# Attention steps queued behind weight splits, and attention heads placed anew among the weight pieces

## The chip, the cores and the metric

The kernel runs on 1 core of one Trainium2 chip. A time is that of one execution of the whole program on the device, in microseconds (us). The kernel before takes 896.84 us as the median of 3 runs (895.47 to 898.17).

The core's engines run side by side, each through its own queue in order: PE does the matmuls (PEld is its weight load), ACT the exponentials, copies and casts, DVE elementwise work and reductions, POOL a little more elementwise work, and SP issues the DMAs.

## The reference

A bidirectional encoder of two layers, for 256 tokens of width 1024, all in float32:

```python
def _token_mixer(xn, w_in, w_pool, pool_scale, w_a, w_b, w_o, rel_bias):
    u, q, k, v, g_pool, g_attn = jnp.split(xn @ w_in, SPLITS, axis=-1)
    # pooling: centred means over 2/4/8/16 tokens, minus the token, times w_pool and a scale
    ...
    # attention: 12 heads of 128 in 3 groups of dilation 1, 4, 16; +-64 strided keys; a bias per head
    ...
    wts = jax.nn.softmax(jnp.stack(lses, axis=0), axis=0)      # groups weighed by their sums
    attn = jnp.einsum('gbsh,gbshd->bshd', wts, jnp.stack(outs, axis=0))
    merged = jax.nn.sigmoid(g_pool) * (pool_out @ w_a) + jax.nn.sigmoid(g_attn) * (attn_out @ w_b)
    return merged @ w_o

def reference(x, ...):
    h = x
    for layer in range(DEPTH):
        h = h + _token_mixer(_rmsnorm(h, norm1[layer]), ...)
        h = h + _conv_ffn(_rmsnorm(h, norm2[layer]), ...)      # width-3 convolution, GELU, gate
    return _rmsnorm(h, norm_f)
```

The weights are float32 and are all read once, 178.68 MB from memory by the profile.

## The kernel before

**Weights in two halves.** Products are made from a high half and a low half of each operand, three matmuls for each block of 128 x 512. A weight is loaded in loads of 1 MB or so into one of three buffers (`raw`), and each load holds two *pieces*. A piece is split: ACT casts its high half, `wh` (L206), and DVE subtracts that from the raw weight, `wl` (L208). There are five buffers for pieces, and a piece takes the one that the piece five before it leaves. `W.get()` hands out the next piece and writes the splits up to three pieces ahead; the load of raw weights behind them is written at once too, on SP's queue (L143). In the stage of this change a piece is used by `by_tokens`, 12 matmuls of 128 x 512 (`v_sum`, L688), and four pieces make one step of 512 columns.

**The order.** The instructions are written in the program's order, but a scheduler places them on each engine: an instruction goes when its inputs are expected, by the scheduler's own costs. Only an edge keeps two in order. `W.after_splits()` gives every instruction of its block an edge to the last high half on ACT and to the last low half on DVE that are written by then (`self.last`). A chip's engine then takes its instructions strictly in the order they were placed.

**The attention between the pieces.** In each layer the projections to queries and keys take 24 pieces, with two of the pooling mixer's among them (numbers 20 to 45 in layer 0), the output of the pooling mixer 8 (46 to 53), the first gate 8 (54 to 61) and the second gate with `w_b` 12 (62 to 73). After each of the 40 pieces of the projections, the pooling output and the first gate `step()` is called, and a table, `steps`, says which parts of the attention are written there. Four *heads* here are the four slots of a group; each slot does its head of all three groups at once:

- `scores(hh)`: for each half of the tokens, matmuls for the near keys (L1054) and for the two strided groups (L1060) into one PSUM tile; DVE scales and adds the bias (L1065) and takes the maximum, negated (`nm`, L1070); ACT does the exponential and its sum (L1073); DVE inverts the sum (L1075) and scales (L1076).
- `start_turn(hh)`: DVE transposes the probabilities in blocks (L735), and SP writes them to memory and reads them back turned (L739, L744).
- `turn(hh)`: ACT and DVE split the turned rows (`pth`, `ptl`: L1096, L1097).
- `weigh(hh)`: 6 matmuls (L1106) and 4 in plain float32 (L1110; the profile shows each of these, and of those of L1060, as two) with the values; ACT and DVE evict the result in two halves (`at2`: L1115, L1116).
- `bring(half)` copies queries out of the rows that came back turned (L1135).

The copies of the pooling mixer's product, `pa` (L1192), and the gates' tanh (L1198) lie between them.

Of the kernel before, what the change touches and what calls it, by code (L numbers as in the profile page):

```python
# [10 lines left out]
F32 = mybir.dt.float32  # L11
F32R = mybir.dt.float32r
AF = mybir.ActivationFunctionType
ALU = mybir.AluOpType
# [7 lines left out]
HD = 128  # L22
# [224 lines left out]
def encoder(ctx, tc, x, w_in, w_pool, pool_scale, w_a, w_b, w_o, norm1, norm2, w_up, conv_w,  # L247
            conv_b, w_down, rel_bias, norm_f, onehot, edges, out):
    nc = tc.nc
# [9 lines left out]
    W = Weights(tc, wpool, big)  # L259

    def cols(w, c0):

        src = w[:, c0 : c0 + 256].rearrange("(k p) c -> p k c", p=P)
        return W.add(
            src, (8, 256), [((lambda t, j=j: t[:, :, j * P : (j + 1) * P]), (8, P)) for j in (0, 1)]
        )
# [26 lines left out]
    for l in range(DEPTH):  # L293
# [37 lines left out]
        for f in range(4, NF, 2):  # L331
            if f in HALF_GROUPS:
                n, j = HALF_GROUPS[f]
                W.use(rows(w_up[l], j * 512, 4, DFF + n * 512, 512))
            a = cols(w_up[l], f * P)
            if f >= 4 * NQ:
                g = cols(w_up[l], DFF + f * P)
                a = [a[0], g[0], a[1], g[1]]
# [107 lines left out]
    def bias_of(t, hh):  # L446

        b = bt[:, hh]
        (pstep, pn), _ = b.ap
        blocks, first = (-2 * P, 4 * P - 1) if t == 0 else (-3 * P, 5 * P - 1)  # L450
        return bass.AP(b.tensor, b.offset + first, [[pstep, pn], [blocks, 2], [-1, 256]])
# [227 lines left out]
    def v_tile():  # L679
        return acc.tile([P, 512], F32, tag="acc", name="v_ps")  # L680
# [248 lines left out]
    for l in range(DEPTH):  # L929
# [25 lines left out]
        else:  # L955
            for g in range(NG):
                held = begun[0] if g == 0 else [W.get() for _ in range(4)]
                for t in range(2):
                    if g + t == 0:
                        ps = begun[1]  # L960
                    else:
                        ps = v_tile()
# [6 lines left out]
        if l == 0:  # L969
            load_params()  # L970
            with tc.issue_after(W.behind[1].ins):
                bias = build_bias()
# [6 lines left out]
        for gi in range(3, -1, -1):  # L979
# [10 lines left out]
            cur, n = u, S + 2 * PAD  # L990
            sh = 1
            while sh < w:
# [3 lines left out]
                    out=nxt[:, :, 0:n], in0=cur[:, :, 0:n], in1=cur[:, :, sh : sh + n]  # L996
# [7 lines left out]
            if hw > 1:  # L1004
# [5 lines left out]
                out=pd, in0=cur[:, :, o : o + S], scalar=1.0 / w, in1=u[:, :, PAD : PAD + S],  # L1010
                op0=ALU.mult, op1=ALU.subtract,
# [37 lines left out]
        def scores(hh):  # L1049
            for t in range(2):  # L1050
                ps = acc.tile([P, 512], F32, tag="acc", name="s_ps")
                ql, kl = (lows[hh // 2][:, j, hh % 2] for j in range(2))
                for m, (a, b) in enumerate(((qh[:, hh], kh[:, hh]), (qh[:, hh], kl), (ql, kh[:, hh]))):
                    nc.tensor.matmul(  # L1054
                        ps[:, 0:256], a[:, t, :], b.rearrange("p t m -> p (t m)"),
                        start=(m == 0), stop=(m == 2),
                    )
                for g in (1, 2):
                    c = 2 * (g - 1) + hh % 2
                    nc.tensor.matmul(  # L1060
                        ps[:, 128 + g * 128 : 256 + g * 128], q[:, hh // 2, c, t, :],
                        kk[:, hh // 2, 4 * t : 4 * t + 4, c, :], start=True, stop=True,
                    )
                s = sm.tile([P, 512], F32, tag="s", name="s")
                nc.vector.scalar_tensor_tensor(  # L1065
                    out=s.rearrange("p (a b) -> p a b", a=2), in0=ps.rearrange("p (a b) -> p a b", a=2),
                    scalar=HD**-0.5, in1=bias_of(t, hh), op0=ALU.mult, op1=ALU.add,
                )
                nm = sm.tile([P, 1], F32, tag="nm", name="nm")
                nc.vector.tensor_reduce(out=nm, in_=s, axis=AX.X, op=ALU.max, negate=True)  # L1070
                z = sm.tile([P, 1], F32, tag="z", name="z")
                p = sm.tile([P, 512], F32, tag="p", bufs=3, name="p")
                nc.scalar.activation(p, s, AF.Exp, bias=nm[:, 0:1], accum_out=z)  # L1073
                rz = sm.tile([P, 1], F32, tag="rz", name="rz")
                nc.vector.reciprocal(rz, z)  # L1075
                nc.vector.tensor_scalar(  # L1076
                    out=p, in0=p, scalar1=rz[:, 0:1], scalar2=0.5, op0=ALU.mult, op1=ALU.mult
                )
                probs[hh, t] = p
# [20 lines left out]
        def weigh(hh):  # L1100
            pth, ptl, pt = ptiles[hh]
            ps = acc.tile([P, 2, P], F32, tag="acc", name="o_ps")
            for kc in range(2):
                c = slice(hh * P, (hh + 1) * P)
                for m, (a, b) in enumerate(((vh, pth), (vh, ptl), (vl, pth))):
                    nc.tensor.matmul(ps, a[:, kc, c], b[:, kc], start=(kc + m == 0), stop=False)  # L1106
            for g in (1, 2):
                hd = (g - 1) * HPG + hh
                for t in range(2):
                    nc.tensor.matmul(  # L1110
                        ps[:, t, :], v[:, t, hd * P : (hd + 1) * P], pt[:, 4 * t : 4 * t + 4, 1 + g, :],
                        start=False, stop=(g == 2 and t == 1),
                    )
            oh, ol = at2[:, hh, 0], at2[:, hh, 1]
            nc.scalar.copy(out=oh, in_=ps)  # L1115
            nc.vector.tensor_sub(out=ol, in0=ps, in1=oh.bitcast(F32))  # L1116

        def parts(which):

# [11 lines left out]
        def bring(half):  # L1131
# [8 lines left out]
            12: ((parts, 1),),  # L1140
            16: ((bring, 0),),
            21: ((scores, 0), (start_turn, 0)),
            24: ((bring, 1),),
            25: ((scores, 1), (start_turn, 1)),
            28: ((turn, 0),),
            29: ((weigh, 0), (scores, 2), (start_turn, 2)),
            32: ((turn, 1),),
            33: ((weigh, 1), (scores, 3), (start_turn, 3)),
            36: ((turn, 2),),
            37: ((weigh, 2),),  # L1150
            38: ((turn, 3),),

            39: ((weigh, 3), (W.load_one, first_up[l][1])),
# [10 lines left out]
        for n in range(6):  # L1164
# [3 lines left out]
            ps = by_tokens(x2, 4, then=step, ahead=pool_out(po2) if n == 1 else None)  # L1168
            y = tmp[:, 1].rearrange("p (t q c j) -> p t q c j", t=2, q=4, c=4)
            if n in (2, 4):  # L1170
                z = tmp[:, 0].rearrange("p (a c j) -> p a c j", a=8, c=4)
            else:

                z = kk[:, (1, 0, None, 0, None, 1)[n]]
# [12 lines left out]
        pa = []  # L1187
        for n in range(2):
            ps = by_tokens(po2, 4, then=step)
            pa.append(big.tile([P, 2, 512], F32, tag=("q0", "k0")[n], name="pa"))  # L1190
            for t in range(2):
                nc.scalar.copy(out=pa[n][:, t], in_=ps[t])  # L1192

        def gate(tag):
            ps = by_tokens(x2, 4, then=step if steps else None)
# [5 lines left out]
        for n in range(2):  # L1201
            th = gate("q1")
            for t in range(2):
                nc.vector.scalar_tensor_tensor(
                    out=pa[n][:, t], in0=th[:, t], scalar=1.0, in1=pa[n][:, t],
                    op0=ALU.add, op1=ALU.mult,
# [8 lines left out]
        for n, cc in enumerate(HALVES):  # L1215
            th = gate("gates")
            ps = by_tokens(at2, 2, 2)
            ks = slice(4 * n, 4 * n + 4)
            y = turned_rows[:, n]
            z = big.tile([P, 2, 4, 4, 32], F32, tag=("q1", "v0")[n], name="merged")  # L1220
            for t in range(2):

                with tc.issue_after((turning if t else made[1]).ins) if n + t else ExitStack():
                    nc.vector.scalar_tensor_tensor(
                        out=th[:, t], in0=th[:, t], scalar=1.0, in1=ps[t], op0=ALU.add, op1=ALU.mult
# [187 lines left out]
```

## Time and profile before

| | |
|---|---|
| median of 3 runs | 896.84 us |
| the profiled execution, its own time | 895.75 us |
| its span, first to last instruction | 893.9 us |
| PE busy | 862.6 us (97%) |
| DVE busy | 658.7 us (74%) |
| ACT busy | 483.9 us (54%) |
| split, DVE (L208), 274 times | 329.1 us, 1216 ns each |
| split, ACT (L206), 274 times | 282.9 us, 1050 ns each |
| mean granted clock of PE | 0.992 |

The page gives the engines' busy times; a view by stretches of time gives the same for any stretch. A timeline lists instructions in order: start, duration, engine, line, operation, output and inputs; `x2` are merged neighbours, and the brackets at the end give how long the engine stood idle before it and what ended that. PE's matmuls are pipelined: one of 128 x 512 lasts about 390 ns while the next starts some 227 ns after it.

### The profile page before, as it was taken

The numbers are of one execution on the slowest core, as the hardware profiler recorded it, in microseconds if no ns is written. First come the engines' busy times: TensorE is split into PE (matmuls) and PEld (weight loads), VectorE is DVE, ScalarE is ACT, GpSimd is POOL, SyncE is SP. The second block draws the span as 40 slices with busy tenths as digits, with TensorE's granted clock in tenths as the row PEclk, the third lists the DMA queues.
The fourth block names the chain that finished last, engine by engine and source line by source line (L and its number), as shares of the span: only waits on it lengthen the run. The fifth ranks groups of instructions, "written<-read, shape, count | busy, mean of one in ns | idle before, by whom it ended". The sixth has DMA issues, their size and how long they took to land.

```text
span 893.9 us, 11515 instructions
## 1 busy us (share of the span) xinstructions
PE 862.6 (97%) x4151; PEld 721.4 (81%) x4151; DVE 658.7 (74%) x1018; ACT 483.9 (54%) x759; POOL 31.0 (3%) x98
## 2 busy tenths in 40 slices
PE   9999997899999999999999999888999999999997
PEld 7888886677888888888888888766778888888886
DVE  7998736655866878989856986374668677888884
ACT  7756524335544565766644664152554464765673
POOL 1800000000010000000000000000000100000000
PEclk9999999999999999999999999999999999999999
DMA  9678675658765777666726578667576568776741
GB/s 329 203 242 274 223 259 163 212 174 279 288 224 189 264 250 262 203 223 232 236 95 219 160 258 282 212 182 240 178 283 226 210 220 273 248 247 214 242 157 47
DMA packets 153089, 199.37 MB, mean 223 GB/s; under 512 B 6905, under 2 KB 101825, under 8 KB 153033
## 3 DMA queue, kind: packets, MB, share of 16 engines
q1 hardware_dynamic: 152872, 198.38, 66.4%
q8 instruction: 32, 0.52, 0.2%
q10 hardware_dynamic: 160, 0.27, 0.1%
q14 instruction: 25, 0.20, 0.1%
HBM read 178.68 MB, written 19.94 MB: 222 GB/s over the span
## 4 chain that ended last, share of the span: by engine, by line
PE 89%; DVE 4%; ACT 3%; DMA 2%; issue 1%; SPq 0%; POOL 0%; POOLq 0%; ACTq 0%; DVEq 0%
PE t_ps L688 40%; PE proj_ps L564 17%; PE v_ps L688 6%; PE res_ps L608 6%; PE res_ps L607 6%; PE res_ps L606 6%; PE v_ps L921 2%; DVE wl L208 2%; PE pool_ps L564 1%; PE v_ps L828 1%; ACT wh L206 1%; DMA turned_p<-turning 1%; PE o_ps L1110 1%; DMA turning<-turning 1%; PE o_ps L1106 1%
## 5 line engine op out<-in xcount | busy, mean ns | idle before, releaser
L208 DVE TENSOR_TENSOR wl<-raw,wh 128x1024 fp32r<-128x1024 f32 x274 | 329.1, 1216 | 82.3 <-ACT wh L206 79.4
L206 ACT CAST wh<-raw 128x1024 fp32r<-128x1024 f32 x274 | 282.9, 1050 | 118.6 <-PE t_ps L688 59.5
L688 PE MATMUL t_ps<-wh,x 128*128 128x512 f32 x960 | 303.2, 393 | 5.7 <-ACT wh L206 5.7
L688 PEld LDWEIGHTS t_ps<-wh,x 128*128 128x128 f32 x960 | 180.9, 189 | 44.2 <-ACT wh L206 6.5
L688 PE MATMUL t_ps<-wl,x 128*128 128x512 f32 x480 | 189.7, 395 | 3.5 <-DVE wl L208 3.5
L688 PEld LDWEIGHTS t_ps<-wl,x 128*128 128x128 f32 x480 | 91.0, 190 | 25.5 <-DVE wl L208 6.7
L564 PE MATMUL proj_ps<-x,wh 128*128 128x512 f32 x448 | 106.5, 390 | 0.0
L564 PEld LDWEIGHTS proj_ps<-x,wh 128*128 128x128 f32 x448 | 83.1, 188 | 16.6
L607 PE MATMUL res_ps<-wl,actq 128*128 128x512 f32 (+1 forms) x184 | 70.0, 380 | 0.0
L608 PE MATMUL res_ps<-wh,actk 128*128 128x512 f32 (+1 forms) x184 | 69.9, 380 | 0.0
L606 PE MATMUL res_ps<-wh,actq 128*128 128x512 f32 (+1 forms) x184 | 69.8, 381 | 0.0
L564 PEld LDWEIGHTS proj_ps<-x,wl 128*128 128x128 f32 x448 | 56.9, 191 | 1.9
L564 PE MATMUL proj_ps<-x,wl 128*128 128x256 f32 x448 | 57.5, 283 | 0.0
L688 PE MATMUL t_ps<-wh,po 128*128 128x512 f32 x128 | 42.7, 408 | 8.2 <-ACT wh L206 8.2
L1065 DVE SCALAR_TENSOR_TENSOR s<-s_ps,bt 128x512 f32<-128x512 f32 x16 | 10.8, 685 | 41.5 <-PE s_ps L1060 41.5
L608 PEld LDWEIGHTS res_ps<-wh,actk 128*128 128x128 f32 x184 | 34.6, 188 | 6.6
L607 PEld LDWEIGHTS res_ps<-wl,actq 128*128 128x128 f32 x184 | 34.6, 188 | 6.4
L606 PEld LDWEIGHTS res_ps<-wh,actq 128*128 128x128 f32 x184 | 34.5, 188 | 6.3
L1073 ACT ACTIVATE p<-s,nm 128x512 f32<-128x512 f32 x16 | 11.6, 725 | 50.6 <-DVE nm L1070 49.6
L688 PEld LDWEIGHTS t_ps<-wh,po 128*128 128x128 f32 x128 | 25.2, 199 | 14.4 <-ACT wh L206 9.4
L1115 ACT CAST at<-o_ps 128x256 fp32r<-128x256 f32 x8 | 3.0, 372 | 52.9 <-PE o_ps L1110 35.0
L475 POOL TENSOR_SCALAR ss<-ss 128x1 f32<-128x1 f32 x8 | 2.0, 254 | 817.6 <-ACT junk L468 817.6
(199 smaller groups left out, 1151.9 us busy)
## 6 DMA issues: line engine op xcount, KB each, us to landing
raw<-in_w_up_dram SPq DMA_DIRECT2D x44, 1024.0 KB, 7.2
raw<-in_w_in_dram SPq DMA_DIRECT2D x34, 1024.0 KB, 5.5
raw<-in_w_in_dram SPq DMA_DIRECT2D x50, 512.0 KB, 4.5
raw<-in_w_down_dram SPq DMA_DIRECT2D x22, 1024.0 KB, 6.0
raw<-in_w_a_dram SPq DMA_DIRECT2D x8, 1024.0 KB
raw<-in_w_o_dram SPq DMA_DIRECT2D x8, 1024.0 KB, 4.9
crossing<-qk_rows SPq DMA_DIRECT2D x12, 512.0 KB, 5.6
crossing<-crossing SPq DMA_DIRECT2D x12, 512.0 KB, 6.0
```

Of the source, the lines that this page charges most:

```text
L206: inst = nc.scalar.copy(out=h, in_=src)
L208: inst = nc.vector.tensor_sub(out=l, in0=src, in1=h.bitcast(F32))
L564: nc.tensor.matmul(out, w(k), x, start=(steps is first and k == 0), stop=(steps is last and k == nk - 1), skip_group_check=turns["rest"],)
L606: nc.tensor.matmul(ps, ah, wh, start=first, stop=False, skip_group_check=on)
L607: nc.tensor.matmul(ps, ah, wl, start=False, stop=False, skip_group_check=on)
L608: nc.tensor.matmul(ps, al, wh, start=False, stop=last, skip_group_check=on)
L688: nc.tensor.matmul(ps, x2[:, 2 * n + j, part, t, :], w[:, j, :], start=(n + m == 0), stop=(n == last and m == 5),)
L828: return nc.tensor.matmul(ps[t], a[:, k, t, :], w[:, k % 2, :], start=first, stop=last)
L921: nc.tensor.matmul(ps[t], a[:, k, t, :], w[:, j, :], start=(k + m == 0), stop=(k == KD - 1 and m == 2),)
L1065: nc.vector.scalar_tensor_tensor(out=s.rearrange("p (a b) -> p a b", a=2), in0=ps.rearrange("p (a b) -> p a b", a=2), scalar=HD**-0.5, in1 ...
L1073: nc.scalar.activation(p, s, AF.Exp, bias=nm[:, 0:1], accum_out=z)
L1106: nc.tensor.matmul(ps, a[:, kc, c], b[:, kc], start=(kc + m == 0), stop=False)
```

## The change

Three kinds of attention instructions now get the edges of `after_splits`: the bias addition, the exponential, and the evictions of the weighing and of `pa`. And the table of `steps` writes scores and weighing at other pieces.

```diff
-                nc.vector.scalar_tensor_tensor(
-                    out=s.rearrange("p (a b) -> p a b", a=2), in0=ps.rearrange("p (a b) -> p a b", a=2),
-                    scalar=HD**-0.5, in1=bias_of(t, hh), op0=ALU.mult, op1=ALU.add,
-                )
+                with W.after_splits():
+                    nc.vector.scalar_tensor_tensor(
+                        out=s.rearrange("p (a b) -> p a b", a=2), in0=ps.rearrange("p (a b) -> p a b", a=2),
+                        scalar=HD**-0.5, in1=bias_of(t, hh), op0=ALU.mult, op1=ALU.add,
+                    )
...
-                nc.scalar.activation(p, s, AF.Exp, bias=nm[:, 0:1], accum_out=z)
+                with W.after_splits():
+                    nc.scalar.activation(p, s, AF.Exp, bias=nm[:, 0:1], accum_out=z)
...
-            nc.scalar.copy(out=oh, in_=ps)
-            nc.vector.tensor_sub(out=ol, in0=ps, in1=oh.bitcast(F32))
+            with W.after_splits():
+                nc.scalar.copy(out=oh, in_=ps)
+                nc.vector.tensor_sub(out=ol, in0=ps, in1=oh.bitcast(F32))
...
-            24: ((bring, 1),),
-            25: ((scores, 1), (start_turn, 1)),
-            28: ((turn, 0),),
-            29: ((weigh, 0), (scores, 2), (start_turn, 2)),
-            32: ((turn, 1),),
-            33: ((weigh, 1), (scores, 3), (start_turn, 3)),
-            36: ((turn, 2),),
-            37: ((weigh, 2),),
+            24: ((scores, 1), (start_turn, 1)),
+            25: ((bring, 1),),
+            27: ((turn, 0),),
+            28: ((weigh, 0), (scores, 2), (start_turn, 2)),
+            30: ((turn, 1),),
+            31: ((weigh, 1), (scores, 3), (start_turn, 3)),
+            35: ((turn, 2),),
+            36: ((weigh, 2),),
             38: ((turn, 3),),
             39: ((weigh, 3), (W.load_one, first_up[l][1])),
...
-                nc.scalar.copy(out=pa[n][:, t], in_=ps[t])
+                with W.after_splits():
+                    nc.scalar.copy(out=pa[n][:, t], in_=ps[t])
```

The line numbers of the attention rise by up to four in the changed kernel (L1073 becomes L1075).

Outside the attention's stretch of each layer every engine's order is the same. Three places in layer 0 follow; layer 1 reads alike.

On ACT, where the scores of heads 0 and 1 are done and the pooling output begins (pieces 46 to 50; `p`, `z` are the probabilities and their sums). Before:

```order
L206 CAST wh45_1299<-raw22_1195 128x1024
L1073 ACTIVATE p_1344,z_1343<-s_1339,nm_1341 128x512
L206 CAST wh46_1315<-raw23_1241 128x1024
L1073 ACTIVATE p_1360,z_1359<-s_1355,nm_1357 128x512
L206 CAST wh47_1374<-raw23_1241 128x1024
L206 CAST wh48_1390<-raw24_1275 128x1024
L206 CAST wh49_1419<-raw24_1275 128x1024
L1073 ACTIVATE p_1465,z_1464<-s_1460,nm_1462 128x512
L1073 ACTIVATE p_1481,z_1480<-s_1476,nm_1478 128x512
L1192 COPY pa_1529<-t_ps_1417 128x512
L1135 COPY q_791<-qk_rows_793 128x1024
L1192 COPY pa_1529<-t_ps_1418 128x512
```

Now:

```order
L206 CAST wh45_1299<-raw22_1195 128x1024
L206 CAST wh46_1315<-raw23_1241 128x1024
L206 CAST wh47_1374<-raw23_1241 128x1024
L206 CAST wh48_1390<-raw24_1275 128x1024
L206 CAST wh49_1419<-raw24_1275 128x1024
L1075 ACTIVATE p_1344,z_1343<-s_1339,nm_1341 128x512
L1075 ACTIVATE p_1360,z_1359<-s_1355,nm_1357 128x512
L1075 ACTIVATE p_1446,z_1445<-s_1441,nm_1443 128x512
L1075 ACTIVATE p_1462,z_1461<-s_1457,nm_1459 128x512
L206 CAST wh50_1476<-raw25_1319 128x1024
L1138 COPY q_791<-qk_rows_793 128x1024
L206 CAST wh51_1495<-raw25_1319 128x1024
```

The casts of pieces 46 to 49 went ahead of all four exponentials, and that of piece 50, which followed the two copies of `pa`, now follows the exponentials directly, ahead of the copies.

On ACT, where head 0 has been weighed and head 2 gets its scores (pieces 53 to 55). Before:

```order
L1096 CAST pth_1550<-turned_p_1049 128x8x2x32
L1115 CAST at2_1416<-o_ps_1572 128x256
L1073 ACTIVATE p_1596,z_1595<-s_1591,nm_1593 128x512
L206 CAST wh54_1554<-raw27_1440 128x1024
L1073 ACTIVATE p_1612,z_1611<-s_1607,nm_1609 128x512
L206 CAST wh55_1626<-raw27_1440 128x1024
```

Now:

```order
L1098 CAST pth_1529<-turned_p_1049 128x8x2x32
L1118 CAST at2_1416<-o_ps_1554 128x256
L1075 ACTIVATE p_1578,z_1577<-s_1573,nm_1575 128x512
L1075 ACTIVATE p_1594,z_1593<-s_1589,nm_1591 128x512
L206 CAST wh54_1608<-raw27_1480 128x1024
L206 CAST wh55_1626<-raw27_1480 128x1024
```

The cast of piece 54 stood between the two exponentials of head 2, and stands behind both now.

On DVE, from the biases of head 1 to the low half of piece 50 (`nm` the maximum, `rz` the inverted sum). Before:

```order
L208 TENSOR_TENSOR wl49_1420<-raw24_1275,wh49_1419 128x1024
L1070 TENSOR_REDUCE nm_1462<-s_1460 128x1
L1065 SCALAR_TENSOR_TENSOR s_1476<-s_ps_1470,bt_82 128x512
L1070 TENSOR_REDUCE nm_1478<-s_1476 128x1
L1075 RECIPROCAL rz_1467<-z_1464 128x1
L1076 TENSOR_SCALAR p_1465<-p_1465,rz_1467 128x512
L1075 RECIPROCAL rz_1483<-z_1480 128x1
L1076 TENSOR_SCALAR p_1481<-p_1481,rz_1483 128x512
L208 TENSOR_TENSOR wl50_1437<-raw25_1319,wh50_1436 128x1024
```

Now:

```order
L208 TENSOR_TENSOR wl49_1420<-raw24_1275,wh49_1419 128x1024
L1066 SCALAR_TENSOR_TENSOR s_1441<-s_ps_1435,bt_82 128x512
L1066 SCALAR_TENSOR_TENSOR s_1457<-s_ps_1451,bt_82 128x512
L1071 TENSOR_REDUCE nm_1443<-s_1441 128x1
L1071 TENSOR_REDUCE nm_1459<-s_1457 128x1
L1077 RECIPROCAL rz_1448<-z_1445 128x1
L1078 TENSOR_SCALAR p_1446<-p_1446,rz_1448 128x512
L1077 RECIPROCAL rz_1464<-z_1461 128x1
L1078 TENSOR_SCALAR p_1462<-p_1462,rz_1464 128x512
L208 TENSOR_TENSOR wl50_1477<-raw25_1319,wh50_1476 128x1024
```

Both biases of head 1 stand behind the low half of piece 49 now; before, the first of them was done ahead of piece 46's.

## The prediction

> **What bounds the kernel now.** I read the page's busy times first, then the stretches of time, then who waited for whom on TensorE (PE), and last the timelines of PE, ScalarE (ACT), VectorE (DVE) and SyncE (SP) around the waits. Pieces of weights are called by their number in the instruction order (`wh50` and `wl50` are the high and low half of piece 50); a time is microseconds from the start of the span, in layer 0.
>
> ```profile
> PE 862.6 (97%) x4151; PEld 721.4 (81%) x4151; DVE 658.7 (74%) x1018; ACT 483.9 (54%) x759; POOL 31.0 (3%) x98
> ...
> 130.00:230.00 100.00, 88.66 (x412) 71.42 (x411) 60.42 (x87) 44.33 (x65) 0.00 (x0) 0.97 0.66 213
> 570.00:670.00 100.00, 88.64 (x413) 71.35 (x412) 59.99 (x86) 44.33 (x65) 0.00 (x0) 0.97 0.66 213
> ...
> 140.00:150.00 10.00, 8.85 (x31) 6.93 (x32) 9.96 (x16) 4.79 (x8) 0.00 (x0) 0.83 0.42 139
> 150.00:160.00 10.00, 7.78 (x33) 5.82 (x32) 5.48 (x9) 7.14 (x10) 0.00 (x0) 1.00 0.75 202
> 170.00:180.00 10.00, 6.63 (x26) 4.99 (x25) 9.33 (x15) 5.82 (x9) 0.00 (x0) 0.83 0.36 134
> ```
>
> PE is the bound: 862.6 of 893.9 us. Its idle time is 31 us, and 22.7 us of that lie in two stretches of 100 us (the columns after the stretch's length are PE, PE weight load, DVE, ACT, POOL, then the granted clock, DMA share and GB/s), one in each layer, where the attention runs between the weight matmuls. DVE is busy 60 and ACT 44 of those 100 us, so neither is short of time: it is a matter of order. The granted clock falls to 0.83 in two slices of 10 us of each stretch.
>
> ```profile
> PE t_ps L688 <- ACT wh L206: 7.9, 4, 2.8
> PE t_ps L688 <- DVE wl L208: 3.4, 7, 0.7
> ...
> 136.12 1.95 PE L1060 MATMUL s_ps<-k,q 128*128 128x128 f32 x16
> 140.48 0.73 PE L688 MATMUL t_ps<-wh,po 128*128 128x512 f32 x2 [2.42 <-ACT wh L206]
> 141.88 0.80 PE L688 MATMUL t_ps<-wl,po 128*128 128x512 f32 x1 [0.66 <-DVE wl L208]
> 145.47 0.62 PE L688 MATMUL t_ps<-wh,po 128*128 128x512 f32 x2
> ...
> 153.65 0.39 PE L688 MATMUL t_ps<-wh,po 128*128 128x512 f32 x1
> 155.74 0.73 PE L688 MATMUL t_ps<-wh,po 128*128 128x512 f32 x2 [1.69 <-ACT wh L206]
> 156.99 0.50 PE L688 MATMUL t_ps<-wl,po 128*128 128x512 f32 x1 [0.52 <-DVE wl L208]
> 157.33 0.63 PE L688 MATMUL t_ps<-wh,po 128*128 128x512 f32 x2
> 165.51 0.28 PE L1106 MATMUL o_ps<-pth,vh 128*128 128x256 f32 x1
> ...
> 169.92 1.05 PE L1060 MATMUL s_ps<-k,q 128*128 128x128 f32 x8
> 173.81 0.73 PE L688 MATMUL t_ps<-wh,x 128*128 128x512 f32 x2 [2.84 <-ACT wh L206]
> 175.07 0.50 PE L688 MATMUL t_ps<-wl,x 128*128 128x512 f32 x1 [0.53 <-DVE wl L208]
> 178.56 0.88 PE L688 MATMUL t_ps<-wh,x 128*128 128x512 f32 x2
> ```
>
> The first two rows are all waits of PE in 130 to 230: 11.3 us, every one for a half of a weight piece, none for the attention itself. Three stops are large. From 157.33 to 165.51 run 36 matmuls without a stop, 0.227 us each, so a piece (12 matmuls) takes 2.73. Stop 1: piece 46 could start at 138.07 and end at 140.80; it ends with the first of the two matmuls at 145.47, about 145.7, so 4.9 are lost, of which the waits are 3.1 and the rest the low clock (0.17 of a slice of 10 us is 1.7). Stop 2: piece 50 could start at 153.88; three of its matmuls are out at 157.33 and nine follow, so it ends at 159.38 instead of 156.61: 2.8 lost, 2.2 as waits, no low clock, 0.3 for each of the two restarts. Stop 3: piece 54 could start at 170.97 and end at 173.70; it ends with the first matmul at 178.56, at about 179.0: 5.3 lost. The other waits are 11.3 - 8.7 = 2.6 in five places; with 0.3 for each restart 4.1. A layer loses about 17.1.
>
> ```profile
> 138.68 0.72 ACT L1073 ACTIVATE p<-s,nm 128x512 f32<-128x512 f32 x1 [16.35 <-DVE nm L1070]
> 139.40 1.03 ACT L206 CAST wh<-raw 128x1024 fp32r<-128x1024 f32 x1
> 152.72 0.59 ACT L1192 COPY pa<-t_ps 128x512 f32<-128x512 f32 x1 [1.83 <-PE t_ps L688]
> 154.63 3.90 ACT L206 CAST wh<-raw 128x1024 fp32r<-128x1024 f32 x4
> 172.01 0.72 ACT L1073 ACTIVATE p<-s,nm 128x512 f32<-128x512 f32 x1 [3.69 <-DVE nm L1070]
> 172.73 1.03 ACT L206 CAST wh<-raw 128x1024 fp32r<-128x1024 f32 x1
> ...
> 136.76 1.29 DVE L1065 SCALAR_TENSOR_TENSOR s<-s_ps,bt 128x512 f32<-128x512 f32 x2 [10.94 <-PE s_ps L1060]
> 137.97 1.27 DVE L1070 TENSOR_REDUCE nm<-s 128x1 f32<-128x512 f32 x2
> 156.86 1.30 DVE L735 STREAM_TRANSPOSE turning<-p 128x512 f32<-128x512 f32 x2
> 158.08 3.46 DVE L208 TENSOR_TENSOR wl<-raw,wh 128x1024 fp32r<-128x1024 f32 x3
> 170.56 0.69 DVE L1065 SCALAR_TENSOR_TENSOR s<-s_ps,bt 128x512 f32<-128x512 f32 x1 [1.78 <-PE s_ps L1060]
> 172.61 0.69 DVE L1070 TENSOR_REDUCE nm<-s 128x1 f32<-128x512 f32 x1
> 175.63 0.45 DVE L1076 TENSOR_SCALAR p<-p,rz 128x512 f32<-128x512 f32 x1
> ```
>
> Each large stop is a cast queued on ACT behind an attention instruction that waits: `wh46` (139.40) behind an exponential that stood 16.35 us for the maximum, `wh50` (154.63) behind the copies of `pa`, which wait for PE's own matmuls, `wh54` (172.73) behind the first exponential of head 2.
>
> **The change, part by part.** It adds and removes no arithmetic; the instruction order differs only in the two attention stretches. DVE steps used below: a low half 1.15 in a row (3.46 for three), bias and maximum 0.64 each in a row, turning a block 0.65, scaling 0.42 when the next starts early.
>
> *Stop 1 goes.* `wh46` to `wh49` now stand ahead of the exponentials and `wl46` ahead of the biases. Their slots come free as pieces 41 to 44 are consumed, before 134, so the casts lie under the matmuls until 138.07. DVE does the biases at 136.76 as before, the maxima to 139.16, `wl47` to 140.35 and `wl48` to 141.5: PE needs `wl47` after piece 46 and two matmuls, at 141.26. It then goes through pieces 46 to 49, from 138.07 to 148.99. Gain 4.9.
>
> *Stop 2 moves.* The exponentials of head 1 now stand ahead of `wh50`, and their biases behind `wl49`. DVE after `wl48`: two reciprocals 0.25, four turnings 2.6 and two scalings 0.85, `wl49` 1.15, two biases 1.28 and two maxima 1.28, hence the last maximum at about 148.8. ACT: the two exponentials start at 148.25 and 149.06 (0.81 with the read of the sum), `wh50` 0.72 after the second, at 149.78, and 1.03 long: PE restarts at 150.86, a wait of 1.87. `wl50` follows to 152.07, so the third matmul comes 1.25 after the first as at 156.99, with a gap of 0.65. Lost: 2.8 (152.12 against 149.44, and 0.1). It was 2.8: no gain and no loss, if the clock stays up as in 150:160.
>
> *Stop 3 grows.* The hold covers only splits that exist when the scores are written; `wh54` is made after them and falls behind both exponentials of head 2. Call T the start of the last score matmuls (169.92 before; 165.05 now, 4.9 earlier). They take 1.05. Before, `wh54` started at T + 2.81. Now the second maximum ends at T + 3.38, as 172.61 + 0.69 says, the second exponential starts at T + 3.42, `wh54` at T + 4.14, and PE at T + 5.22: a wait of 4.17 instead of 2.84. `wl54` comes behind the second scaling and the second turning, at T + 5.7, and the third matmul at T + 6.95 instead of T + 5.15. Behind T + 1.05 + 0.45 that is 5.45, with 0.1 and the low clock (1.7, as at 2.84) 7.25; it was 5.3. Loss 2.0.
>
> *The rest.* From piece 55 on I placed the same steps: all halves are ready before PE needs them, except `wl58`, which stands behind two scalings and two turnings of head 3 and comes 0.35 late, 0.65 with the restart. The five small stops had cost 4.1: gain 3.4. What hides the moved evictions is the distance to the weighing: the closest is head 2, where the low half of the probabilities (now behind `wl59` and the two products with the gate) ends at 191.2 and PE comes to it at 191.3. If that cover goes, each 1 us late costs PE 1 us.
>
> ```profile
> 145.13 0.42 SPq L143 DMA_DIRECT2D raw<-in_w_a_dram  x1
> 155.33 1.78 SPq L744 DMA_DIRECT2D k<-crossing  x4
> 158.19 0.38 SPq L739 DMA_DIRECT2D turning<-turning  x1
> 165.83 1.80 SPq L744 DMA_DIRECT2D turned_p<-turning  x4
> ...
> DMA to landing us min/median/max: 3.4/4.4/5.0
> ...
> DMA to landing us min/median/max: 5.5/5.5/5.5
> ```
>
> The first landing row is that of the turned rows (`turned_p`), the second that of the raw loads from 118 to 200.
>
> *Queues.* On SP a load of raw weights moves behind each turning of heads 1 to 3. Head 1's rows are turned at 153.35, while SP still issues the keys to 157.1, so that the load for piece 54 goes at 157.6 where it went at 157.21 and lands (5.5) at 163, six before its cast. The turned rows of head 1 go by 166.6 even if the 7.6 between 158.19 and 165.83 stays; they land by 171.6 (5.0), and PE asks for them at 177.5. Cost nothing; loads of pieces 58 and 62 go at 171.2 and 187.5 and have seven and more to spare.
>
> *Sum.* A layer: 4.9 + 0 - 2.0 + 3.4 = 6.3; two layers, since 570:670 repeats 130:230, about 13. The profiled execution took 895.75 (span 893.9); the median, 896.84, is 1.1 above it, and carries over: 896.84 - 13 = **883.8 us**.
>
> *The clock.* The 0.83 after a wait of 2.42 and one of 0.66, against 1.00 after 1.69 and 0.52, puts the fall between these; the new 1.87 and 0.65 are nearer the second, so I charge none there and 1.7 at stop 3. Bounds: 0 and 1.7 at either stop. The Trainium skill, "TensorE: Matmul & The Clock Gate", section Part 1: The HAM clock gate (the "warmup" mystery), has the clock halve after an idle window of about 3.4 us and return after a busy one, the windows running free of the program. By that length the new stop 2 would cost nothing and stop 3 the half clock, which is the sum above; yet it would also have spared stop 1, and the trace shows 0.83 there, so the row decides. That the windows run free would make it a matter of where they fall; this is the first rival below.
>
> **The rivals.** *The low clock comes at stop 2 as well* (chance 0.2): two points, 1.69 without and 2.42 with the low clock, do not tell where between them it turns, and 1.87 is between. 1.7 in each layer: 883.8 + 3.4 = 887.2.
>
> *Stop 3 does not grow, and stop 2 neither loses* (0.12): the score matmuls of head 2 end with other work in front that I charged twice, and the small stops were worth the whole floor. Without the 2.0 of stop 3 in both layers: 879.8. Against it: the order of ACT is fixed, and both exponentials stand ahead.
>
> *The stop goes on down the line* (0.08): heads 2 and 3 are weighed with almost no slack (0.1 and 1.4). If the gates' tanh or the turned rows come 2 late, each of the two weighings stops 1 to 2 us and brings the low clock back once; with stop 2's 1.7 that is 3 + 1.7 + 1.7 = 6.4 a layer, all of the gain: 896.6, the same. For it: these steps now wait for PE's own last matmul of a gate. Against it: in 130:230 no wait of PE is for the attention.
>
> *Slower* (0.05): raw loads starve behind the turnings. SP issues in order; three loads a layer now stand behind a turning that waits for DVE. The spare is 6 to 9 us. From a delay of 9 PE waits for each of the three; to lose the gain of 6.3 each must come 2.1 later still, and 14 late would cost 3 x 5 - 6.3 = 8.7 a layer, 914. For it: the stretch before waited 7.6 from turning to turned rows. Against it: turnings end within 6 us of their scores here.
>
> *That the change does nothing* is excluded by the order of ACT: the casts of 46 to 49 do stand ahead.
>
> **How the numbers follow.** The forecast has 0.55: 881 to 886 for single errors of half a microsecond at its ten places. With the rivals: 0.2 at 887, 0.12 at 880, 0.08 at about 896, 0.05 above. The range 877 to 891 leaves out the last two and a little of the edges; of the rival at 896 a quarter falls below the bound of faster. About 0.3% (2.7 us) is what a measurement of this kernel can tell from no change: faster than 894.1 by 0.89, within 0.06, slower 0.05.
>
> **What would show it.** In the profile after: no wait of PE at 138; a wait of about 1.9 for `wh` at 149 and one of about 4.2 at 166, the latter followed by the only slice at 0.83; PE idle near 8 instead of 11.3 in each stretch; the wait of ACT's exponential for the maximum still there, but with no cast behind it that PE needs, save those two. Wrong if PE waits on o_ps, or for a raw load, if the slice after 150 shows 0.83, or if the stop at 166 is below 3.

## The result, and the profile after

The changed kernel takes 882.79 us as the median of 4 runs (882.18 to 884.58), the kernel before 896.19 beside it (895.47 to 898.17): 0.985 of the time, 95% interval 0.983 to 0.987. Predicted were 883.8, within 877 to 891. The profiled execution has a span of 881.5 us, 12.4 less than before.

From the page of the changed kernel, and from its view by stretches (the columns are those of the view before):

```profile
PE 860.3 (98%) x4151; PEld 723.4 (82%) x4151; DVE 660.2 (75%) x1018; ACT 485.9 (55%) x759; POOL 31.9 (4%) x98
...
130.00:230.00 100.00, 93.22 (x441) 77.36 (x440) 66.63 (x91) 46.43 (x68) 0.00 (x0) 0.95 0.72 230
570.00:670.00 100.00, 93.22 (x433) 77.12 (x432) 69.92 (x96) 47.58 (x69) 0.00 (x0) 0.93 0.73 237
...
150.00:160.00 10.00, 9.47 (x35) 7.33 (x34) 6.12 (x7) 4.85 (x7) 0.00 (x0) 0.83 0.73 202
170.00:180.00 10.00, 8.60 (x38) 6.89 (x39) 5.37 (x8) 3.01 (x4) 0.00 (x0) 0.72 0.78 242
580.00:590.00 10.00, 8.14 (x28) 5.95 (x27) 9.25 (x14) 7.73 (x12) 0.00 (x0) 0.83 0.80 241
600.00:610.00 10.00, 5.09 (x13) 3.45 (x13) 9.08 (x14) 4.98 (x8) 0.00 (x0) 0.61 0.48 160
```

PE idles 6.8 us of each attention stretch where it idled 11.3. The granted clock is lower than before, though: 0.95 and 0.93 over the stretches instead of 0.97, with dips at both stops that are left, in both layers. So part of PE's gain in idle time was paid back as slow matmuls.

PE's waits in 130 to 230, and its timeline around the places of the three stops:

```profile
PE t_ps L688 <- ACT wh L206: 5.5, 2, 4.2
PE t_ps L688 <- DVE wl L208: 1.3, 2, 0.8
...
137.12 0.71 PE L688 MATMUL t_ps<-wh,po 128*128 128x512 f32 x2
...
149.63 0.73 PE L688 MATMUL t_ps<-wh,po 128*128 128x512 f32 x2 [1.34 <-ACT wh L206]
...
170.65 1.22 PE L688 MATMUL t_ps<-wh,x 128*128 128x512 f32 x2 [4.16 <-ACT wh L206]
172.62 0.79 PE L688 MATMUL t_ps<-wl,x 128*128 128x512 f32 x1 [0.76 <-DVE wl L208]
```

Piece 46 starts at 137.12 right behind the score matmuls: stop 1 is gone, and so are all small stops (the two rows of waits are two stops and nothing else). Stop 2 has shrunk from 1.69 to 1.34, stop 3 has grown from 2.84 to 4.16. DVE and ACT ahead of stop 2:

```profile
138.46 2.35 DVE L208 TENSOR_TENSOR wl<-raw,wh 128x1024 fp32r<-128x1024 f32 x2
...
145.16 1.28 DVE L1066 SCALAR_TENSOR_TENSOR s<-s_ps,bt 128x512 f32<-128x512 f32 x2
146.36 1.26 DVE L1071 TENSOR_REDUCE nm<-s 128x1 f32<-128x512 f32 x2
...
147.12 0.73 ACT L1075 ACTIVATE p<-s,nm 128x512 f32<-128x512 f32 x1 [7.62 <-DVE nm L1071]
148.55 1.03 ACT L206 CAST wh<-raw 128x1024 fp32r<-128x1024 f32 x1
```

ACT's exponential still stands 7.62 us for the maximum, but the only cast behind it that PE needs is that of piece 50 (148.55).

A simple measure of a layer is the stretch from the start of head 1's score matmuls to the first residual matmul behind the attention. The rows that end it in layer 0, before, and those that begin and end it now:

```profile
241.80 0.39 PE L606 MATMUL res_ps<-wh,m 128*128 128x512 f32 x1
```

```profile
135.42 1.95 PE L1060 MATMUL s_ps<-k,q 128*128 128x128 f32 x16
...
234.67 0.39 PE L606 MATMUL res_ps<-wh,m 128*128 128x512 f32 x1
```

In layer 0 it went from 105.7 us (136.12 to 241.80) to 99.3 (135.42 to 234.67): 6.4 less, where 6.3 were predicted. Layer 1 gave 5.1 (105.7 to 100.6), and 0.7 had been won before layer 0's attention: 12.2 of the 12.4. The second executions of both kernels, further down, give 4.7 in layer 0 (105.2 to 100.5) and 5.4 in layer 1 (104.3 to 98.9), so the close match in layer 0 is in part the luck of one execution.

### The profile page after: what moved, and what is told of

The parts are those of the page before. It is cut to its first block, busy times and chain, and to the rows that moved or that the text cites. A ratio compares the mean times of both kernels' runs of the same rounds, so it can differ in the third digit from the quotient of the medians.

```text
span 881.5 us, 11523 instructions
## 1 busy us (share of the span) xinstructions
PE 860.3 (98%) x4151; PEld 723.4 (82%) x4151; DVE 660.2 (75%) x1018; ACT 485.9 (55%) x759; POOL 31.9 (4%) x98
## 4 chain that ended last, share of the span: by engine, by line
PE 93%; DVE 5%; ACT 1%; issue 1%; POOL 0%; POOLq 0%; ACTq 0%; DVEq 0%
PE t_ps L688 43%; PE proj_ps L564 18%; PE v_ps L688 6%; PE res_ps L608 6%; PE res_ps L606 6%; PE res_ps L607 6%; PE v_ps L921 2%; PE v_ps L828 1%; DVE wl L208 1%; PE pool_ps L564 1%; DVE s L1066 1%; PE o_ps L1112 1%; PE s_ps L1054 1%; PE o_ps L1108 1%; DVE nm L1071 1%
## 5 line engine op out<-in xcount | busy, mean ns | idle before, releaser
L1119 DVE TENSOR_TENSOR at<-o_ps,at 128x256 fp32r<-128x256 f32 x8 | 3.4, 425 | 37.5 <-ACT at L1118 37.5
L1350 ACT CAST actq<-g 128x256 fp32r<-128x256 f32 x44 | 17.0, 404 | 20.7 <-DVE g L1339 20.0
```

What stands on the lines that cost most here:

```text
L1350: nc.scalar.copy(out=ah, in_=g)
```

## The experiments

All ratios are against the kernel before on the same chip (medians of 895.3 to 896.7). Theory A: the holds make the gain, and the new places in the table take some of it back, since the holds then cover one split less. B is its rival in the expectations of each run.

### The two halves of the change

The holds with the old table:

```diff
-            24: ((scores, 1), (start_turn, 1)),
-            25: ((bring, 1),),
...
+            24: ((bring, 1),),
+            25: ((scores, 1), (start_turn, 1)),
...
```

> The holds of the change, with the table of steps of the kernel before. Theory A (the holds make the gain, and the new table costs, since heads 1 and 2 are written one piece earlier and so the hold covers one split less): the casts of pieces 50 and 54 now stand ahead of the exponentials of heads 1 and 2, so stop 2 (1.34 and 0.53 in the changed kernel) and stop 3 (4.16 and 0.76) both go; 22 to 24 us less than the changed kernel over two layers, with at most 2 us given back in each layer at piece 54, whose raw load is then only just in time: 860 to 866. Theory B (the holds need the new table, which keeps scores and weighing apart): the stops stay and the weighings wait: 885 to 895.

Measured: 869.9 us (869.6 to 871.6), ratio 0.971 (0.968 to 0.974). Stops of this run in layer 0, and its stretch:

```profile
162.76 0.73 PE L688 MATMUL t_ps<-wh,x 128*128 128x512 f32 x2 [0.45 <-ACT wh L206]
205.94 0.74 PE L688 MATMUL t_ps<-wh,at 128*128 128x512 f32 x2 [1.18 <-ACT wh L206]
...
130.00:230.00 100.00, 96.22 (x467) 79.77 (x466) 70.34 (x98) 50.05 (x72) 0.00 (x0) 1.00 0.75 247
```

The holds alone win twice what the whole change wins. Stops 1 and 2 are gone, of stop 3 0.45 and 0.53 us are left at piece 54, and the clock stays at 1.00. The size fell 4 us short of A's range, because small stops (0.3 to 1.2 us) turn up further on.

The new table without the holds, at all four places:

```diff
-                with W.after_splits():
-                    nc.scalar.activation(p, s, AF.Exp, bias=nm[:, 0:1], accum_out=z)
+                nc.scalar.activation(p, s, AF.Exp, bias=nm[:, 0:1], accum_out=z)
...
```

> The new table of steps, without any hold. Theory A: stop 1 stays as in the kernel before (2.42 and 0.66), stop 2 stays (its cast waits behind the copies of the pooling product), stop 3 grows to 4.2 and 0.8 as in the changed kernel, the small stops stay: the time before plus 4, about 900. Theory B (the new table makes the gain): 883 to 888.

Measured: 901.9 us (898.5 to 904.0), ratio 1.005 (1.003 to 1.007): slower. The timeline of this run:

```profile
156.93 0.73 PE L688 MATMUL t_ps<-wh,po 128*128 128x512 f32 x2 [1.62 <-ACT wh L206]
...
176.34 0.73 PE L688 MATMUL t_ps<-wh,x 128*128 128x512 f32 x2 [4.15 <-ACT wh L206]
178.31 0.80 PE L688 MATMUL t_ps<-wl,x 128*128 128x512 f32 x1 [1.24 <-DVE wl L208]
```

The stop of 4.15 at piece 54 is there without any hold: it is the table's, which brings the scores of head 2 one piece earlier. Added to the holds the table costs 12.9 us (882.8 against 869.9), alone 5.2: A stands.

### The evictions

The change without the holds on the evictions (`pa` and the weighing's two halves):

```diff
-            with W.after_splits():
-                nc.scalar.copy(out=oh, in_=ps)
-                nc.vector.tensor_sub(out=ol, in0=ps, in1=oh.bitcast(F32))
+            nc.scalar.copy(out=oh, in_=ps)
+            nc.vector.tensor_sub(out=ol, in0=ps, in1=oh.bitcast(F32))
...
-                with W.after_splits():
-                    nc.scalar.copy(out=pa[n][:, t], in_=ps[t])
+                nc.scalar.copy(out=pa[n][:, t], in_=ps[t])
```

> The change without the holds on the evictions of the weighing and of the pooling product. Theory A: one copy of the pooling product, which waits for PE's last matmul of piece 49, falls ahead of the exponentials of head 1 on ACT, and the cast of piece 50 behind them and the second copy: PE waits about 4.6 at piece 50 instead of 1.34; stop 3 as in the changed kernel: 888 to 892. Theory B (the holds on evictions do nothing, since they move no split that PE needs): 883, as the changed kernel.

Measured: 894.6 us (893.1 to 897.7), ratio 0.9985 (0.9968 to 1.0003), no difference from before. Its timeline:

```profile
150.56 0.73 PE L688 MATMUL t_ps<-wh,po 128*128 128x512 f32 x2 [2.38 <-ACT wh L206]
...
171.38 0.73 PE L688 MATMUL t_ps<-wh,x 128*128 128x512 f32 x2 [4.16 <-ACT wh L206]
...
212.56 0.73 PE L688 MATMUL t_ps<-wh,x 128*128 128x512 f32 x2 [1.18 <-ACT wh L206]
```

Without the evictions' holds stop 2 is 2.38 instead of 1.34; theory A had expected about 4.6 there, and 888 to 892 for the whole. The holds are worth 11.8 us (894.6 against 882.8), most of the change's whole gain, and more than A gave them. Stop 2 is the smaller part of it: in layer 0 the way from head 1's score matmuls to piece 54 takes 36.1 us where the changed kernel takes 35.2, but from there to the first residual matmul 69.3 where the changed kernel takes 64.0 (65.4 in its layer 1). Behind piece 54 the small stops are back, the largest at 212.56: on ACT the eviction of the weighing stands 5.72 us for PE's sums and goes at 211.19, and the cast that PE needs stands right behind it, at 211.46. In the changed kernel that cast goes ahead of the eviction. So copies that wait for PE's own matmuls are as bad a thing to stand ahead of a cast as an exponential.

### The split that the holds don't cover

The change, with two more splits written ahead of every head's scores; then for head 2 alone:

```diff
         def scores(hh):
+            W._split(W.n_got + 5)
```

> The change, and the scores first have two more pieces split, so that the hold covers five pieces in place of three. Theory A: the casts of 50 and 51 stand ahead of the exponentials of head 1, those of 54 to 56 ahead of head 2's: stops 2 and 3 go, as in the kernel with the old table: 858 to 866; the cast of 54 still stands behind the eviction of head 0's weighing and may cost 1 us in each layer. Theory B (the third stop is the chain from the scores to the exponential itself, which PE meets in the weighing): PE waits for the weighing of heads 1 to 3 in place of a cast, 875 or more.

Measured: 871.7 us (871.2 to 872.5), ratio 0.972 (0.970 to 0.975).

```diff
         def scores(hh):
+            if hh == 2:
+                W._split(W.n_got + 5)
```

> The change, with two more splits issued ahead at the start of head 2's scores alone, so that its exponentials stand behind them too; head 1 as in the change. Theory A (each stop is a cast behind a waiting exponential, and the two stops are independent): stop 3 goes (7.2 us in layer 0, 9.1 in layer 1), stop 2 stays with its 1.34 and 0.53 and its low clock; the run with both heads moved left 3 to 5 us a layer in small stops after piece 54, which come here too: 882.8 - 16.3 + 8 = 874 (871 to 877). Theory B (the stop goes on down the line with the work): a wait above 2 us turns up at a piece behind 54, and the time is 880 to 886.

Measured: 871.3 us (870.7 to 872.4), ratio 0.973 (0.970 to 0.975). From the second of these runs:

```profile
149.57 0.73 PE L688 MATMUL t_ps<-wh,po 128*128 128x512 f32 x2 [1.34 <-ACT wh L206]
...
167.18 0.73 PE L688 MATMUL t_ps<-wh,x 128*128 128x512 f32 x2 [0.80 <-ACT wh L206]
```

One step for head 2 takes stop 3 from 4.16 to 0.80, leaves stop 2 as it was, and brings 11.5 us, what moving both heads brings (11.1). So stop 3 is a cast behind two exponentials and nothing else; the wait above 2 us that theory B expected behind it does not turn up. In the run with both heads stop 2 is gone too, yet the time is the same: its stops further on (0.3 to 0.8 us) make up for it. That run missed A's range (858 to 866) by 6.

### The clock by itself

PE kept at work while it waits: 6 extra matmuls ahead of piece 50, 18 ahead of piece 54, on PE alone.

```diff
+        for k in range(busy):
+            with tc.issue_after(last_mm[busy > 6]):
+                nc.tensor.matmul(ps[0], x2[:, 0, 0, 0, :], x2[:, 0:4, 0, 0, :], start=(k == 0), stop=False)
...
-            ps = by_tokens(po2, 4, then=step)
+            ps = by_tokens(po2, 4, then=step, busy=(0, 6)[n])
...
-            th = gate("q1")
+            th = gate("q1", (18, 0)[n])
```

> The change, with TensorE kept at work while it waits: 6 extra 128x512 matmuls stand ahead of piece 50's first matmul and 18 ahead of piece 54's, in each layer, added into the tile that the piece sums into (so two tiles of gate and pooled values hold a wrong sum; nothing else of the work differs, and the orders of ScalarE and VectorE are the changed kernel's). At the 0.23 us that a 128x512 matmul takes in a row of them, 6 take 1.4 us against the wait of 1.34, and 18 take 4.1 against 4.16. Theory C: the low clock is the answer to the idle stretch itself. Then the waits of 1.34 and 4.16 read below 0.3, the slices from 150 to 180 us show 1.00, and each stop costs its waits alone: stop 2 falls from 3.8 (layer 0) and 4.1 (layer 1) to about 1.9, stop 3 from 7.2 and 9.1 to about 4.9, together 10.5 us less: 872 (870 to 875). Theory D: the low clock has another cause (the load of the engines together, or the moment), and idle time only happens to stand beside it. Then the slices still show 0.7 to 0.9, the extra matmuls run at half rate too and push piece 50 and 54 back: 883 to 890.

Measured: 877.2 us (876.0 to 881.1), ratio 0.980 (0.977 to 0.983). Slices and timeline of this run (L704 are the extra matmuls, L690 those of the pieces):

```profile
150.00:160.00 10.00, 9.47 (x43) 7.63 (x42) 6.02 (x7) 4.75 (x7) 0.00 (x0) 1.00 0.70 207
170.00:180.00 10.00, 9.12 (x54) 8.07 (x55) 5.57 (x8) 3.35 (x6) 0.00 (x0) 1.00 0.94 307
...
148.03 1.52 PE L704 MATMUL t_ps<-po 128*128 128x512 f32 x6
149.53 0.73 PE L690 MATMUL t_ps<-wh,po 128*128 128x512 f32 x2
164.50 4.38 PE L704 MATMUL t_ps<-x 128*128 128x512 f32 x18
168.91 0.73 PE L690 MATMUL t_ps<-wh,x 128*128 128x512 f32 x2
```

The clock is 1.00 in all of both stretches, though PE's useful work waits as long as before, and its mean is 0.998 or 0.999 in each of the four executions (0.985 to 0.990 in the changed kernel's): with PE at work there is no low clock. The extra products go into the sums of two tiles, so what this version computes is no longer the encoder; it serves for its time alone. From piece 50 to piece 54 it now takes 19.38 us (149.53 to 168.91) where the changed kernel takes 21.02 (149.63 to 170.65): the low clock of stop 2 costs 1.6. The layer stretches are 2.6 and 4.0 shorter, so that of stop 3 costs 1.0 in layer 0 (2.6 less the 1.6 of stop 2) and, in the same way, 2.4 in layer 1. Theory C holds in kind, not in size: of its 10.5 us the stretches show 6.6 and the medians 5.6, and the time lies 2 above its range. A part of that is the wait for the low half of piece 54, which is 1.24 here and 0.76 in the changed kernel, where slow matmuls fill some of it. The profiled execution (881.1) holds one further stop of 2.1 and 0.5 in the second layer's last part; the other three took 876.0 to 877.4.

Three extra matmuls at stop 2 alone:

```diff
-            ps = by_tokens(po2, 4, then=step)
+            ps = by_tokens(po2, 4, then=step, busy=(0, 3)[n])
```

> The change, with 3 extra 128x512 matmuls (0.23 us each, 0.7 together) ahead of piece 50's first matmul alone, so that 1.34 us of idle time become about 0.65, with the 0.53 behind it as before (one tile of pooled values holds a wrong sum; nothing else differs). The run with 6 of them had no low clock and saved 1.6 us a layer there. Theory E (the idle time itself, in some short stretch, decides): 0.65 + 0.53 is less than the 1.18 + 0.53 that left the clock at 1.00 in the run of the holds alone, so the slices from 150 to 160 and from 580 to 590 show 1.00, and 1.6 a layer are saved: 879.6 (878 to 881). Rival F (the length of the idle time has little to do with it, the moment decides): the slices still show 0.83 and the time stays at 882 to 884.

Measured: 880.8 us (879.4 to 881.6), ratio 0.983 (0.980 to 0.985). Its rows:

```profile
149.36 0.73 PE L690 MATMUL t_ps<-wh,po 128*128 128x512 f32 x2 [0.66 <-ACT wh L206]
...
150.00:160.00 10.00, 9.47 (x42) 7.77 (x42) 5.84 (x7) 4.58 (x7) 0.00 (x0) 1.00 0.68 210
580.00:590.00 10.00, 8.82 (x38) 6.63 (x37) 8.68 (x13) 7.73 (x12) 0.00 (x0) 1.00 0.78 235
```

With 0.66 and 0.53 idle the clock stays up in both layers, as theory E expects, and piece 50 to piece 54 takes 19.4 us in both. By itself this is weak evidence, as the next two runs show.

The changed kernel and the kernel before, each profiled a second time, with no edit:

> The changed kernel once more, for a second profiled execution. If the low clock hangs on where an idle stretch falls among windows that run free of the program, stop 2 (1.34 and 0.53) shows 1.00 in one layer or the other this time, with a span about 1.6 us shorter for each; if it hangs on the program alone, 0.83 stands again in 150 to 160 and in 580 to 590, and the span is 881 to 882.

> The kernel before once more, for a second profiled execution. If the moment among free windows decides, stop 2 (1.69 and 0.52, clock at 1.00 in both layers of the first profile) shows 0.83 in some layer, and stops 1 and 3 may show 1.00 in one; if the program alone decides, the slices read as in the first profile: 0.83, 1.00 and 0.83 at 140, 150 and 170.

Measured: 882.4 and 894.7 us, one execution each. The changed kernel's second execution:

```profile
170.10 0.73 PE L688 MATMUL t_ps<-wh,x 128*128 128x512 f32 x2 [4.16 <-ACT wh L206]
...
235.46 0.39 PE L606 MATMUL res_ps<-wh,m 128*128 128x512 f32 x1
...
150.00:160.00 10.00, 9.59 (x35) 7.79 (x36) 5.64 (x7) 4.37 (x7) 0.00 (x0) 0.83 0.70 197
580.00:590.00 10.00, 8.14 (x35) 6.10 (x34) 9.23 (x14) 7.73 (x12) 0.00 (x0) 1.00 0.84 245
...
584.32 0.74 PE L688 MATMUL t_ps<-wh,po 128*128 128x512 f32 x2 [1.33 <-ACT wh L206]
...
603.69 0.73 PE L688 MATMUL t_ps<-wh,x 128*128 128x512 f32 x2 [4.16 <-ACT wh L206]
```

The kernel before, first execution and then second:

```profile
580.87 0.73 PE L688 MATMUL t_ps<-wh,po 128*128 128x512 f32 x2 [2.42 <-ACT wh L206]
...
580.00:590.00 10.00, 8.47 (x30) 6.59 (x31) 9.97 (x16) 5.18 (x8) 0.00 (x0) 0.83 0.40 128
```

```profile
580.97 0.73 PE L688 MATMUL t_ps<-wh,po 128*128 128x512 f32 x2 [2.42 <-ACT wh L206]
...
580.00:590.00 10.00, 8.36 (x35) 6.60 (x36) 9.95 (x16) 5.22 (x8) 0.00 (x0) 1.00 0.40 129
```

In layer 1 of the changed kernel stop 2 had 0.83 in the first execution and has 1.00 in the second, after the same 1.33 us. In layer 1 of the kernel before, stop 1 has 1.00 after the same 2.42 that brought 0.83 the first time. Same program, same stop, another clock: the moment has a part in it. What was expected beside it, 0.83 at stop 2 of the kernel before in some layer, did not come: it shows 1.00 in both layers again.

The price of that low clock shows once more: from piece 50 to piece 54 layer 1 of the changed kernel took 20.95 us (583.54 to 604.49) and takes 19.37 now (584.32 to 603.69), 1.6 less. At stop 1 of the kernel before it was 1.4: from head 1's scores to piece 54 layer 1 took 37.7, and takes 36.3. Layer 0 of the changed kernel is 1.3 longer the second time, all of it behind piece 54: 65.4 us to the first residual matmul (170.10 to 235.46) where the first execution took 64.0 (170.65 to 234.67). Layer 1 took 65.4 there the first time and 65.3 the second, and with the extra matmuls it was 63.0, so the low clock of stop 3 cost 1.0 in one case of four and 2.3 to 2.4 in three.

### Versions that go further

The change with splits written ahead of scores and weighing; then the holds with the old table and the same, with one split ahead (`+ 4` in place of `+ 5`), and with two:

```diff
         def scores(hh):
+            W._split(W.n_got + 5)
...
         def weigh(hh):
+            W._split(W.n_got + 5)
```

> The run that issued two more splits ahead of every head's scores (871.7), and the same two ahead of the weighting too, so that the evictions of its sums stand behind more splits as well. That run's largest stops left are 0.8 us at the pieces that the weighting is written beside. Theory A: those stops go as well, 2 to 3 us a layer: 866 (863 to 869). Rival: the weighting's sums are evicted later, the bank that they hold comes free later, and PE waits for it: above 872.

Measured: 865.4 us (864.4 to 865.7), ratio 0.966 (0.963 to 0.968).

> The holds with the old table (869.9 when run alone), and one more split issued ahead at the start of each head's scores and weighting. In the run of the holds alone the stops left were 0.45 + 0.53, 0.81, 0.29 and 1.18 + 0.52 in layer 0, 3.8 us a layer. Theory A: they shrink or go, 865 (862 to 868). Rival: what is left comes from the total of the splitting engines' work in this stretch, not from its order, and the stops only move: 868 to 872.

Measured: 867.9 us (867.5 to 869.5), ratio 0.969 (0.967 to 0.971): on the border between A's range and the rival's.

> The holds with the old table, and two more splits issued ahead at the start of each head's scores and weighting; with one more it took 867.9, and its largest wait left was 1.3 us for a low half beside the weighting of head 2, in both layers. Theory A (what is left is still order): that wait goes too, 865.5 (864 to 867), level with the new table with two ahead (865.4). Rival: what is left is the sum of the splits and attention steps that DVE has in that place, and an order behind more splits only makes the attention late: 868 or more.

Measured: 862.5 us (860.6 to 863.0), ratio 0.962 (0.959 to 0.965). Of the run with one ahead the largest stop left, and of the run with two the stretches:

```profile
187.68 0.50 PE L688 MATMUL t_ps<-wl,x 128*128 128x512 f32 x1 [1.27 <-DVE wl L208]
```

```profile
130.00:230.00 100.00, 99.44 (x487) 83.56 (x485) 72.53 (x101) 50.85 (x73) 0.00 (x0) 1.00 0.77 258
570.00:670.00 100.00, 99.21 (x484) 83.04 (x483) 72.39 (x99) 50.82 (x75) 1.07 (x3) 1.00 0.80 266
```

The last is the fastest: PE is idle for 0.6 of 100 us, at full clock, and 20.3 us are gone beside the changed kernel. What was left was order, not the amount of work: the rival that expected 868 or more fell, and A's range was beaten by 1.5. Its waits on the attention itself stay small; of PE in 130 to 230:

```profile
PE o_ps L1110 <- DVE ptl L1100: 0.3, 1, 0.3
PE t_ps L688 <- ACT pa L1198: 0.2, 1, 0.2
```

These two are all that is left there: for the low half of turned probabilities, and for a PSUM bank that the later copy of `pa` gives back.

## Why the prediction was right, and where it was wrong

The sum was right to about a microsecond, partly because its errors cancel and partly by luck, since the low clock of one stop moves a layer by 1.3 to 1.6 us between executions of the same program. By terms, of the first execution where no other is named:

- **Stop 1 goes (+4.9 a layer).** Right. PE starts piece 46 at 137.12 without a wait, and the holds do it: in the run of the holds alone the stop is gone, in the run of the table alone it is there.
- **Stop 2 moves (0).** Wrong in two sizes. The wait was 1.34 by the profile, and 1.49 if it is counted as in the prediction, from the moment at which the next matmul could have started (148.14), instead of 1.87: the steps of DVE from the end of `wl48` to the last maximum took 6.8 us (140.8 to 147.62), and I had counted 7.3, each step a little too long (the four turnings 2.6 instead of 2.44, from start to start). And the clock did fall.
- **The clock: "I charge none there and 1.7 at stop 3".** This is the step that failed; the sign I had named for it, 0.83 in the slice after 150, came. It rested on the reading that a length between 1.69 and 2.42 us parts the cases. In the changed kernel the low clock came after 1.34 and 0.53, and in the second execution of the kernel before it stayed away after 2.42 and 0.66. Length alone doesn't decide. Its price of 1.7 was nearly right at stop 2 (1.6); at stop 3 it was 1.0 and 2.4.
- **Stop 3 grows (7.25 lost).** Right in layer 0: waits of 4.16 and 0.76 against 4.17 and 1.0, 7.2 lost. The mechanism is shown by the run that moved only head 2's splits. In layer 1 the low clock reached on into piece 55, and about 9 were lost.
- **The rest (+3.4).** A little low: `wl58` is not late, so all 4.1 of the small stops went. The moved evictions cost nothing, as said; left out of the hold they would have cost 11.8 for the whole kernel, which I had not worked out.
- **The sum.** In layer 0, by the stops: 4.9 - 1.0 (stop 2: 3.8 lost instead of 2.8) - 1.9 (stop 3) + 4.1 = 6.1, and 6.4 measured. In layer 1 the same account gives 4.9 - 1.3 - 3.8 + 4.1 = 3.9 and 5.1 were measured; 1.2 of it I can't place, most of which lies behind the start of piece 54. The 0.7 before the attention lies at the start of the program: among the waits of the kernel before stands

```profile
PE xt_ps L776 <- DMA h<-in_x_dram: 0.9, 1, 0.9
```

for the input, and the changed kernel's profile has no such wait. No edit touches that place, and the second execution of the kernel before has no such wait either and comes to head 1's scores 0.4 earlier (135.70). In the four executions of the two kernels these scores start between 134.94 and 136.12, so the 0.7 is not shown to be the change's.

The likeliest rival (low clock at stop 2 as well, 887.2) thus had the right event, but not its reason, for it put the turn between 1.69 and 2.42 and the clock fell after 1.34. Its time is too long, in part because the shorter wait at stop 2 (about 0.4 a layer) and the last small stop (0.65 a layer) came in beside it. Of the others nothing showed: PE waits neither on `o_ps` nor for raw loads.

The rule of the Trainium skill that was weighed there ("TensorE: Matmul & The Clock Gate", section Part 1: The HAM clock gate (the "warmup" mystery)) has two parts. That the windows run free of the program agrees with the two pairs of executions above. That an idle window of about 3.4 us is needed does not agree: PE stood still for 1.34 and 0.53 us with 0.73 of matmuls between, and the clock fell. What share of which window is needed stays open; stops of 1.69 and 0.52 kept the full clock in both layers and both executions, and I have no run that explains it.

## What to carry to other kernels

Look at what stands behind a waiting instruction on its engine: a cast that could have gone earlier cost PE 2.8 to 5.3 us at each of the three stops, because an exponential or an eviction ahead of it waited for another engine. A hold covers only the work that is written by then, so write that work first and place the hold after it; each such step has to be tried apart, for here one half of the change won 27 us and the other gave 13 back. And a short stop of PE costs more than its length: price it with and without the low clock behind it (here 1.0 to 2.4 us), since which of them comes can change between executions.

## What the runs showed that was not expected

- The granted clock after the same stop of the same program differs between executions: 0.83 and 1.00 after 1.33 us in layer 1 of the changed kernel, 0.83 and 1.00 after 2.42 in layer 1 of the kernel before.
- Extra matmuls in a wait pay: 24 a layer, about 5.9 us of matmuls that the encoder has no use for, made the kernel 5.6 us faster than the same without them (877.2 against 882.8), since they keep the clock at 1.00. Here they go into the sums of two tiles; a version that keeps them out of the result was not run.
- The place of the evictions in the queues of ACT and DVE decides over 11.8 us, though no matmul of PE waits for their results in the profile of either kernel (in the kernel before two weight loads waited for `pa`, 0.6 us in all).
